# The first group of a transformer block's input projection, taken block by block of 128 channels

## The chip, the cores and the metric

The kernel runs on one core of a Trainium2 chip. The metric is the device time of one execution in microseconds. The kernel before took 1697.79 us (median of three runs, 1696.65 to 1697.9).

## The reference

One layer of an encoder block for 256 tokens of 2048 channels, in float32. Cut to what the change touches:

```python
mod = silu(c) @ w_ada + b_ada                   # 2048 -> 6 * 2048, one vector
sh1, sc1, gt1, sh2, sc2, gt2 = split(mod, 6)
h = rmsnorm(x, g_pre_mix) * (1.0 + sc1) + sh1   # 256 x 2048
proj = h @ w_in                                 # 2048 -> 10752 columns
lb = cumsum(softmax(hg_lb_logits))              # "bounds" of the forget gates
cos, sin = rotary angles of the positions       # "sines"
y = mixer(proj, lb, cos, sin)                   # gated recurrence, windowed attention, output projection
x = x + gt1 * rmsnorm(y, g_post_mix)
x = x + gt2 * rmsnorm(expert_ffn(x), g_post_ffn)  # 16 experts, each picks 32 tokens
```

## The kernel before

**Weights.** All weights come through one queue, SP's, in tiles of 128 x 2048 floats (1 MB), in the order of the list `prog` and, behind it, of the experts. `take()` (L156 to L161) issues one tile into the next free slot of a pool of 27 slots; six of these are a ring for split weights. A slot that is still read holds up the queue.

**Modulation.** `silu(c)` is spread over all partitions as a row, CR (`expand`, L293). A tile ("A", p, k) or ("B", p, k) of w_ada gives part p (0 shift, 1 scale, 2 to 5 the others) of the 128 channels of block k, by one VectorE instruction (`ada`, L398 to L401). `mod_gain` (L403) adds bias and gain.

**h.** `norm_x` (L317) squares x, scales its rows on ScalarE, turns it by 32 TensorE transposes and copies the blocks to NTl. `make_h(g)` (L411) makes h of four blocks: for each block one ScalarE instruction with scale and shift (L417), a cast to the rounded high part HH (L418), and on VectorE the low part HL, the difference (L419).

**Products.** Ten "early" chunks of 512 columns of w_in, f0 b0 f1 b1 q0 q1 hg0 hg1 v0 v1, are taken in four groups of four channel blocks each (GRP). For each chunk and group a tile ("W", ...) comes; `split` (L426 to L438) casts its two halves on ScalarE (L434) and takes the differences on VectorE (L435). `prod` (L440) issues 48 matmuls for a chunk and a group, three for each pair of block and 128 columns: high by high, high by low, low by high. The sum stands in one of two halves of PSUM (`big`, used in turn). In groups 2 to 4 ScalarE first copies the sum so far back into PSUM (L788, "reload"), and after a chunk it copies the sum out (L791, "eviction"; in group 4 L793 with a sigmoid or silu, which needs another function table). So a chunk can start only when the chunk two before has been evicted and its own sum reloaded. After the early chunks come the late chunks of w_in and the recurrence (`hgrn`), then attention, output projection, routing and the experts.

**What sets the order.** The queues of SP, and of ScalarE, VectorE and TensorE, each run their instructions in the order that a list scheduler of the framework wrote at build time; it moves instructions freely within the data dependences. `pairs` holds extra dependences that pin one instruction behind another. In the kernel before only a few are pinned: group 1's h on ScalarE, and the second square. All eight w_ada tiles of group 1 stand ahead of the first w_in tile in `prog`, then two B tiles are mixed into each group (`BE = [2, 2, 2, 10]`). Bounds and sines are computed at the very start.

Of the kernel before, what the change touches and what calls it, by code (L numbers as in the profile page):

```python
# [14 lines left out]
F32 = mybir.dt.float32  # L15
# [4 lines left out]
ALU = mybir.AluOpType  # L20
# [6 lines left out]
H = 8  # L27
NE = 16
FF = 1024
SMW = 160  # L30
# [12 lines left out]

# [81 lines left out]
def block_kernel(ctx: ExitStack, tc: tile.TileContext, x, cols, pos, ident_in, hmask, smask, w_ada, w_in, w_a, w_b, w_out, w_r, w_gu, w_dn, out):  # L125
# [35 lines left out]
        return t  # L161

    pairs = []

    def latest(engine):
        for i in reversed(nc.cur_bb.bb.instructions):
# [61 lines left out]

    NG = len(GRP)
    G0 = [sum(GRP[:g]) for g in range(NG)]  # L230
    prog = [("X",)]
    a_tiles = [("A", p, k) for k in range(KT) for p in range(2)]
    b_tiles = [("B", p, k) for p in range(2, 6) for k in range(KT)]
    prog += a_tiles[:2 * GRP[0]]
    for g in range(NG):
        todo = b_tiles[:BE[g]]
        b_tiles = b_tiles[BE[g]:]
        if g < NG - 1:
            todo = a_tiles[2 * G0[g + 1]:2 * G0[g + 1] + 2 * GRP[g + 1]] + todo
# [12 lines left out]
    def mix(items, plan):

# [26 lines left out]
    stream += [src(it) for it in prog if it[0] not in "HX"]  # L280
# [33 lines left out]
    V.tensor_tensor(sig, sig, col("c"), ALU.mult)  # L314
    CR = expand(sig, "crow")
    crow_done = latest(mybir.EngineType.Activation)
    X = [mem.get([D], F32, "x") for _ in range(NT)]  # L317
    ssq = tiny(NT)

    def norm_x():  # L320
        for tt in range(NT):
            nc.sync.dma_start(X[tt], x[tt])
        scr = mem.get([D], F32, "sq")
        for tt in range(NT):
            S.activation(scr, X[tt], AF.Square, accum_out=ssq[:, tt:tt + 1])
        pairs.append((latest(mybir.EngineType.Activation), crow_done))
        mem.put(scr)
        rs = rsqrt(ssq, NT)
        for k2 in range(8):
            if k2 % 2 == 0:  # L330
                for tt in range(NT):
                    xp = X[tt][:, 256 * k2:256 * k2 + 512]
                    S.activation(xp, xp, AF.Copy, scale=rs[:, tt:tt + 1])
            b = bank()
            for j in range(2):
                for tt in range(NT):
                    E.transpose(b[:, 256 * j + 128 * tt:256 * j + 128 * tt + 128],
                                X[tt][:, 128 * (2 * k2 + j):128 * (2 * k2 + j) + 128], ident)
            S.copy(NTl[k2 // 4][:, 2 * (k2 % 4):2 * (k2 % 4) + 2, :].rearrange("p a b -> p (a b)"), b)
        mem.put(*X)  # L340

    def load_masks():
        mtmp = mem.get([2, 128], F32, "mtmp")
# [15 lines left out]
    table()  # L359
    S.activation(le, le, AF.Exp)  # L360
    ls3 = lsum.rearrange("p (d h) -> p d h", d=2)
    V.tensor_tensor(ls3, le4[:, :, 0, :], le4[:, :, 1, :], ALU.add)
    V.reciprocal(lsum, lsum)
    V.tensor_tensor(LB, le4[:, :, 0, :], ls3, ALU.mult)
    V.tensor_scalar(OM, LB, -1.0, 1.0, ALU.mult, ALU.add)
    V.tensor_scalar(NOM, LB, 1.0, None, ALU.subtract)


    CS = cp.tile([128, 2, NT, 64], F32, name="CS")
# [1 line left out]
    def rotary():  # L371
        w = mem.get([4, 128], F32, "rot")
        ang, n_, t_ = w[:, 0, :], w[:, 1, :], w[:, 2, :]
        pf = tiny(NT)
        V.tensor_copy(pf, posi)
        for tt in range(NT):
            V.tensor_scalar(ang[:, 64 * tt:64 * tt + 64], col("inv"), pf[:, tt:tt + 1], None, ALU.mult)
        for sc in (4096.0, 1.0):
            magic = 12582912.0
            V.tensor_scalar(n_, ang, 1.0 / (2 * math.pi * sc), magic, ALU.mult, ALU.add)  # L380
            V.tensor_scalar(n_, n_, magic, None, ALU.subtract)
            for cc in (6.28125, 1.9350051879882812e-3, 3.0199159819567e-07):
# [15 lines left out]
    def ada(p, k, t):  # L398

# [11 lines left out]
    def make_h(g):  # L411
        ks = slice(G0[g], G0[g] + GRP[g])
        mod_gain(0, ks)
        mod_gain(1, ks)
        for kt in range(ks.start, ks.stop):
            n = hk(NTl, kt)
            S.activation(n, n, AF.Identity, scale=MOD[:, 1, kt:kt + 1], bias=MOD[:, 0, kt:kt + 1])  # L417
            S.copy(hk(HH, kt), n)  # L418
            V.tensor_tensor(hk(HL, kt), n, hk(HH, kt).bitcast(F32), ALU.subtract)  # L419
            if kt % 2:  # L420
                yield
        if g == NG - 1:
            mem.put(*NTl)


    def split(t):  # L426
# [430 lines left out]
    LA = LAH  # L857
    pend = []
    hs, hg_ = iter(()), 0
    for it in prog:  # L860
        if it[0] == "H":
            hs, hg_ = make_h(it[1]), it[1]
            if it[1] == 0:
                n, p = len(nc.cur_bb.bb.instructions), latest(mybir.EngineType.Activation)
                for _ in hs:
                    pass
                pairs += [(i, p) for i in nc.cur_bb.bb.instructions[n:] if i.engine == mybir.EngineType.Activation]
            continue
        if it[0] == "X":
            norm_x()  # L870
            rotary()
            continue
        t = take()
        if it[0] in "AB":
# [5 lines left out]
            if it == ("B", 4, KT - 1):  # L880
                router_consts()
        else:
            pend.append((it, split(t)))
            if it[0] == "W" and it[2] < G0[hg_]:
                next(hs, None)
            else:
                for _ in hs:
                    pass
# [398 lines left out]
```

## Time and profile before

| | |
|---|---|
| Time, median of three runs | 1697.79 us |
| Time of the profiled execution | 1695.95 us |
| Its span, first to last instruction | 1694.2 us |
| TensorE busy (matmul) | 1415.6 us, 84% |
| VectorE, ScalarE busy | 778.0 us, 554.1 us |
| DMA | 633.58 MB, mean 374 GB/s |

The span has three stretches. From 36 to about 740 us TensorE is nearly always busy with the products of the mixer; from about 750 us to the end the DMA engines are, with the experts' weights; ahead of 36 us TensorE waits for the first w_in tile. A share of busy time says little here: the change lies in the first 36 us and in the order of the ScalarE instructions up to 270 us, so single rows of the timeline are read.

### The profile page before, as it was taken

The page shows a single profiled execution, that of the slowest core. Times are in us where ns is not written, and L with a number is a line of the kernel's source. Part 1 is how long each engine was busy: PE and PEld are TensorE (multiplying, and loading weights), DVE is VectorE, ACT ScalarE, POOL GpSimd, SP SyncE. Part 2 cuts the span into 40 slices and gives each one's busy share as a digit, 9 for nine tenths or more (in the row PEclk, how much of TensorE's full clock was granted, in tenths as well). Part 3 has the DMA queues.
Part 4 walks back from the last instruction along what each step waited for, and adds up shares of the span by engine and source line. Part 5 has one row for each costly group of instructions (what it writes and reads, how often), then busy time and mean ns, then how long its engine had stood idle before and what let it go on. Part 6 is the DMA issues. An engine that isn't in the chain of part 4 may idle for free.

```text
span 1694.2 us, 22085 instructions
## 1 busy us (share of the span) xinstructions
PE 1415.6 (84%) x9162; PEld 864.6 (51%) x9162; DVE 778.0 (46%) x1070; ACT 554.1 (33%) x854; POOL 0.2 (0%) x4
## 2 busy tenths in 40 slices
PE   4999999999999999979876777776776777677776
PEld 3999997787888888853321221231222232122122
DVE  8788879989878799751111111110111111111113
ACT  6577777765675444432110100010000010001013
POOL 0000000000000000000000000000000000000000
PEclk7999999999999999998998878888987987888789
DMA  9999976665778879989999999999999999999996
GB/s 383 419 419 385 361 308 227 257 236 201 291 277 324 353 283 385 420 358 419 418 419 419 420 419 420 419 419 419 419 419 420 420 419 420 419 419 419 420 420 268
DMA packets 88372, 633.58 MB, mean 374 GB/s; under 512 B 10064, under 2 KB 10448, under 8 KB 11472
## 3 DMA queue, kind: packets, MB, share of 16 engines
q1 hardware_dynamic: 87984, 631.39, 91.8%
q8 instruction: 72, 1.18, 0.3%
q10 hardware_dynamic: 288, 0.79, 0.1%
q14 instruction: 28, 0.23, 0.0%
HBM read 630.04 MB, written 2.10 MB: 373 GB/s over the span
## 4 chain that ended last, share of the span: by engine, by line
PE 46%; DMA 46%; DVE 5%; ACT 2%; issue 1%; SPq 0%; ACTq 0%; DVEq 0%
PE PS L178 45%; DMA w<-in_w_gu_dram 33%; DMA w<-in_w_dn_dram 11%; DVE hl L435 1%; DMA w<-in_w_in_dram 1%; DMA w<-in_w_ada_dram 1%; ACT ew L1117 1%; DVE w L400 1%; DVE F L508 0%; PE PS L915 0%; PE PS L1090 0%; PE PS L686 0%; ACT ew L1087 0%; DVE T L514 0%; ACT hl L434 0%
## 5 line engine op out<-in xcount | busy, mean ns | idle before, releaser
L178 PE MATMUL PS<-w,rt 128*32 128x512 f32 x2048 | 314.4, 692 | 144.2 <-DMA w<-in_w_gu_dram 143.2
L435 DVE TENSOR_TENSOR hl<-w,hl 128x1024 fp32r<-128x1024 f32 x232 | 278.6, 1223 | 86.4 <-ACT hl L434 85.6
L178 PE MATMUL PS<-hl,hl 128*128 128x256 f32 (+1 forms) x928 | 309.3, 335 | 0.0
L434 ACT CAST hl<-w 128x1024 fp32r<-128x1024 f32 x232 | 237.7, 1049 | 151.5 <-PE PS L178 142.7
L178 PE MATMUL PS<-hl,hh 128*128 128x512 f32 x832 | 270.1, 399 | 0.7 <-ACT hl L434 0.6
L178 PEld LDWEIGHTS PS<-w,rt 128*32 128x32 f32 x2048 | 54.6, 115 | 349.0 <-DMA w<-in_w_gu_dram 283.9
L400 DVE SCALAR_TENSOR_TENSOR w<-w,crow 128x2048 f32<-128x2048 f32 x96 | 219.1, 2286 | 3.8 <-DMA w<-in_w_ada_dram 3.8
L1128 DVE TENSOR_TENSOR acc<-acc,PS 128x512 f32<-128x512 f32 x120 | 82.6, 688 | 274.2 <-PE PS L178 274.2
L178 PE MATMUL PS<-ew,rt 128*128 128x256 f32 x512 | 157.3, 434 | 60.3 <-ACT ew L1117 60.3
L178 PE MATMUL PS<-hh,hl 128*128 128x256 f32 x1024 | 186.3, 285 | 8.7 <-ACT hh L418 8.7
L178 PEld LDWEIGHTS PS<-hl,hl 128*128 128x128 f32 x928 | 177.5, 191 | 16.3 <-issue 1.0
L178 PEld LDWEIGHTS PS<-hl,hh 128*128 128x128 f32 x832 | 155.6, 188 | 33.3 <-ACT hl L434 1.0
L178 PE MATMUL PS<-w,ew 128*32 128x256 f32 x2048 | 153.2, 422 | 18.1 <-DVE ew L1096 15.4
L178 PEld LDWEIGHTS PS<-hh,hl 128*128 128x128 f32 x1024 | 161.2, 193 | 9.2 <-ACT hh L418 9.1
L178 PEld LDWEIGHTS PS<-ew,rt 128*128 128x128 f32 x512 | 94.8, 206 | 136.2 <-ACT ew L1117 121.1
L1117 ACT COPY ew<-PS 128x256 f32<-128x256 f32 x128 | 47.5, 371 | 281.4 <-PE PS L178 281.4
L1096 DVE TENSOR_TENSOR ew<-ew,PS 128x256 f32<-128x256 f32 x16 | 6.8, 422 | 230.7 <-ACT ew L1095 230.7
L178 PEld LDWEIGHTS PS<-w,ew 128*32 128x32 f32 x2048 | 57.1, 116 | 92.5 <-issue 47.4
L1087 ACT COPY ew<-PS 128x512 f32<-128x512 f32 x16 | 9.4, 585 | 226.4 <-PE PS L178 226.4
L178 PE MATMUL PS<-hl,mh 128*128 128x512 f32 x256 | 80.2, 393 | 0.0
L1051 DVE TENSOR_SCALAR rt<-ct,rt 128x128 f32<-128x128 f32 x32 | 9.6, 343 | 123.6 <-PE PS L1055 123.6
L991 DVE TENSOR_SCALAR rt<-ct,rt,small 128x32 f32<-128x32 f32 x32 | 9.4, 300 | 105.0 <-PE PS L178 104.8
(251 smaller groups left out, 1104.7 us busy)
## 6 DMA issues: line engine op xcount, KB each, us to landing
w<-in_w_gu_dram SPq DMA_DIRECT2D x256, 1024.0 KB, 19.9
w<-in_w_dn_dram SPq DMA_DIRECT2D x128, 1024.0 KB, 19.9
w<-in_w_ada_dram SPq DMA_DIRECT2D x96, 1024.0 KB, 9.0
w<-in_w_in_dram SPq DMA_DIRECT2D x84, 1024.0 KB, 7.3
w<-in_w_out_dram SPq DMA_DIRECT2D x16, 1024.0 KB, 14.6
w<-in_w_a_dram SPq DMA_DIRECT2D x8, 1024.0 KB, 7.4
w<-in_w_b_dram SPq DMA_DIRECT2D x8, 1024.0 KB, 8.2
x<-in_x_dram SPq DMA_DIRECT2D x4, 1024.0 KB, 12.4
```

Of the source, the lines that this page charges most:

```text
L178: E.matmul(o, l, r, start=start, stop=stop, skip_group_check=True, **kw)
L400: V.scalar_tensor_tensor(t, t, 1.0, CR, ALU.mult, ALU.mult, accum_out=MOD[:, p, k:k + 1])
L434: S.copy(hl[:, 0, :], w)
L435: V.tensor_tensor(hl[:, 1, :], w, hl[:, 0, :].bitcast(F32), ALU.subtract)
L991: V.tensor_scalar(oh[:, tt, :], io, pm3[:, tt, e:e + 1], r2[:, tt:tt + 1], ALU.is_equal, ALU.mult)
L1051: V.tensor_scalar(rp[:, tt], io[:, None, :].to_broadcast([128, 4, 32]), pm3[:, tt, e:e + 1], aff[:, tt, e:e + 1], ALU.is_equal, ALU.mult)
L1087: S.copy(gu, b)
L1096: V.tensor_tensor(he, sl_, b3[:, :, 64:128], ALU.mult)
L1117: S.copy(EW[:, 2, 256 * (cb % 2):256 * (cb % 2) + 256], b[:, :256])
L1128: V.tensor_tensor(acc(cb), acc(cb), p3, ALU.add)
```

## The change

The first group is written out by hand in a new function `start()`: for each block k of 128 channels the two w_ada tiles come, h of this block is made (`h_hi` on ScalarE, `h_lo` on VectorE), and the products of two chunks, f0 and b0, for this block follow (`products`), 12 matmuls per block and chunk. Their two w_in tiles stand as the third and sixth of the ten tiles; in the kernel before f0's was the ninth and b0's the eleventh. Both PSUM halves are in use for it. All instructions of `start()` on VectorE, ScalarE and TensorE are pinned in the order in which they are written. The bounds and sines move to the first chunk of group 2 ("R"), pinned behind the instructions that stand ahead there. One ScalarE table load goes at the start; `Abs` becomes a VectorE instruction. The B tiles go from 2, 2, 2, 10 to 0, 2, 2, 12 per group, and h of group 2 is made one chunk later (NH0).

```diff
-BE = [2, 2, 2, 10]
+BE = [0, 2, 2, 12]
-NH0 = 3
+NH0 = [2, 3, 3]
+    def behind(n, last):
+        for i in nc.cur_bb.bb.instructions[n:]:
+            if i.engine in last and "DMA" not in str(i.opcode):
+                pairs.append((i, last[i.engine]))
-    prog += a_tiles[:2 * GRP[0]]
+    NS = 2
+    begin = []
+    for k in range(GRP[0]):
+        begin += a_tiles[2 * k:2 * k + 2]
+        if k < NS:
+            begin.append(("W", EARLY[k], 0, GRP[0]))
...
+        names = EARLY[NS:] if g == 0 else EARLY
+        nt, ne = len(todo), len(names)
+        m = ne - 1 if g == 0 else ne
+        for i, n in enumerate(names):
             prog.append(("W", n, G0[g], GRP[g]))
+            k = min(nt, (i + 1) * nt // m) - min(nt, i * nt // m)
...
+            if g < NG - 1 and i == ne - NH0[g]:
                 prog.append(("H", g + 1))
+            if g == 1 and i == 0:
+                prog.append(("R",))
...
+    def start():
+        n0 = len(nc.cur_bb.bb.instructions)
...
+            S.copy(CR[:, 512 * c:512 * c + 512], b)
+            if c == 0:
+                S.activation(PS[:, 0:2048], X[0], AF.Square, accum_out=ssq[:, 0:1])
...
+        def h_hi(k):
+            S.activation(MOD[:, 0, k:k + 1], MOD[:, 0, k:k + 1], AF.Identity, bias=bada[:, 0, k:k + 1])
+            S.activation(MOD[:, 1, k:k + 1], MOD[:, 1, k:k + 1], AF.Identity, scale=col("gpm")[:, k:k + 1],
+                         bias=gb[:, k:k + 1])
+            n = hk(NTl, k)
+            S.activation(n, n, AF.Identity, scale=MOD[:, 1, k:k + 1], bias=MOD[:, 0, k:k + 1])
+            S.copy(hk(HH, k), n)
+        def h_lo(k):
+            V.tensor_tensor(hk(HL, k), hk(NTl, k), hk(HH, k).bitcast(F32), ALU.subtract)
+        acc = [big(), big()]
+        def products(i, k):
+            hl, _ = mod[i][k // 2]
+            j = k % 2
+            wh, wl = hl[:, 0, 512 * j:512 * j + 512], hl[:, 1, 512 * j:512 * j + 512]
+            ah, al = hk(HH, k), hk(HL, k)
+            for c in range(4):
+                o, cs = acc[i][:, 256 * c:256 * c + 256], slice(128 * c, 128 * c + 128)
+                mm(o, wh[:, cs], ah, k == 0 and c % 2 == 0, False)
+                mm(o, wl[:, cs], ah, False, False)
+                mm(o, wh[:, cs], al, False, k == 3)
...
+        one()
+        rs = rsqrt(ssq, NT, lambda: S.activation(le, le, AF.Exp))
+        scaled(0)
+        one()
+        one()
+        turn_x(0)
+        h_hi(0)
+        scaled(1)
+        turn_x(1)
+        one()
+        h_lo(0)
+        products(0, 0)
+        one()
+        one()
+        h_hi(1)
+        h_lo(1)
+        products(0, 1)
+        products(1, 0)
+        products(1, 1)
+        scaled(2)
+        turn_x(2)
+        scaled(3)
+        turn_x(3)
+        mem.put(*X)
+        one()
+        one()
+        h_hi(2)
+        one()
+        h_lo(2)
+        products(0, 2)
+        products(1, 2)
+        one()
+        h_hi(3)
+        h_lo(3)
+        products(0, 3)
+        products(1, 3)
+        new = nc.cur_bb.bb.instructions[n0:]
+        for e in (mybir.EngineType.DVE, mybir.EngineType.Activation, mybir.EngineType.PE):
+            own = [i for i in new if i.engine == e and "DMA" not in str(i.opcode)]
+            pairs.extend((i, p) for p, i in zip(own, own[1:]))
+            ends[e] = own[-1]
+        for i in range(NS):
+            S.copy(slab(EARLY[i]), acc[i])
...
+        if it[0] == "R":
+            n, last = len(nc.cur_bb.bb.instructions), {e: latest(e) for e in ends}
+            bounds()
+            next(rot)
+            behind(n, last)
             continue
```

`one()` takes the next tile: a w_ada tile for `ada`, a w_in tile for `split`. `scaled(c)` scales 512 columns of both halves of x on ScalarE, `turn_x(c)` transposes them (8 transposes on TensorE, two ScalarE copies to NTl).

The pins hold instructions of `start()` to each other, but others may come between them: on VectorE the first w_ada tile of group 2 stands ahead of the last `h_lo(3)`. The change also moves the scheduler's order further on, in three places.

The first is the turn from group 1 to group 2. On VectorE before: hl_567, hl_570 are the split of hg1, hl_628, hl_631 that of v0, the w tiles between are w_ada's, and MOD rows add bias and gain for group 2.

```order
L435 TENSOR_TENSOR hl_567<-w_565,hl_567 128x1024
L435 TENSOR_TENSOR hl_570<-w_565,hl_570 128x1024
L400 SCALAR_TENSOR_TENSOR w_623,MOD<-w_623,crow_89 128x2048
L405 TENSOR_TENSOR MOD<-MOD,ct 128x4
L407 SCALAR_TENSOR_TENSOR MOD<-MOD,ct 128x4
L435 TENSOR_TENSOR hl_628<-w_626,hl_628 128x1024
L435 TENSOR_TENSOR hl_631<-w_626,hl_631 128x1024
```

After, on VectorE: hl_620, hl_623 are the split of v0, hl_684, hl_687 that of v1.

```order
L548 TENSOR_TENSOR hl_620<-w_618,hl_620 128x1024
L548 TENSOR_TENSOR hl_623<-w_618,hl_623 128x1024
L395 SCALAR_TENSOR_TENSOR w_676,MOD<-w_676,crow_101 128x2048
L400 TENSOR_TENSOR MOD<-MOD,ct 128x4
L395 SCALAR_TENSOR_TENSOR w_679,MOD<-w_679,crow_101 128x2048
L400 TENSOR_TENSOR MOD<-MOD,ct 128x4
L402 SCALAR_TENSOR_TENSOR MOD<-MOD,ct 128x4
L548 TENSOR_TENSOR hl_684<-w_682,hl_684 128x1024
L548 TENSOR_TENSOR hl_687<-w_682,hl_687 128x1024
```

Two w_ada tiles instead of one stand ahead of the last MOD row, and this comes one chunk later, ahead of v1's split. On ScalarE before, at the same turn: Q_78 holds the sums of q0 and v0, Q_85 those of q1 and v1, F_52 those of f0 and b0; the casts are of v1 (hl_698, hl_701), f0 (hl_764, hl_767) and b0 (hl_800, hl_803), the last two for group 2.

```order
L434 CAST hl_698<-w_696 128x1024
L434 CAST hl_701<-w_696 128x1024
L791 COPY Q_78_512<-PS 128x1024
L788 COPY PS<-F_52_270 128x1024
L434 CAST hl_764<-w_762 128x1024
L434 CAST hl_767<-w_762 128x1024
L791 COPY Q_85_573<-PS 128x1024
L788 COPY PS<-F_52_270 128x1024
L434 CAST hl_800<-w_798 128x1024
L434 CAST hl_803<-w_798 128x1024
```

After, on ScalarE: Q_70 is the tile of q0 and v0, Q_77 that of q1 and v1, F_40 that of f0 and b0, hl_799 and hl_802 are b0's casts, L413 is the cast of h, L382 and L383 are the sines.

```order
L904 COPY Q_70_504<-PS 128x1024
L413 CAST hh_83<-nT_81 128x256
L382 ACT_TABLE_LOAD
L382 ACTIVATE CS<-rot_120 128x128
L383 ACTIVATE CS<-rot_120 128x128
L904 COPY Q_77_565<-PS 128x1024
L547 CAST hl_799<-w_797 128x1024
L547 CAST hl_802<-w_797 128x1024
L901 COPY PS<-F_40_350 128x1024 x2
```

The reload of f0's sum, which stood right behind v0's eviction, now stands behind v1's eviction and b0's two casts.

The second place is group 4, on ScalarE, around the eviction of q0. Before: hl_2177 and hl_2180 are the casts of q1, Q_78 is q0's sum.

```order
L793 ACTIVATE F_65_391<-PS 128x1024
L788 COPY PS<-Q_85_573 128x1024
L434 CAST hl_2177<-w_2175 128x1024
L434 CAST hl_2180<-w_2175 128x1024
L793 ACT_TABLE_LOAD
L793 ACTIVATE Q_78_512<-PS 128x1024
```

After: hl_2179 and hl_2182 are the casts of q1, Q_70 is q0's sum.

```order
L906 ACTIVATE F_57_383<-PS 128x1024
L901 COPY PS<-Q_77_565 128x1024
L906 ACT_TABLE_LOAD
L906 ACTIVATE Q_70_504<-PS 128x1024
L547 CAST hl_2179<-w_2177 128x1024
L547 CAST hl_2182<-w_2177 128x1024
```

The casts of q1 now stand behind the eviction of q0, the chunk right before it.

The third place is the end of group 4 on ScalarE. Before: Q_85 is v1's sum, hl_2486 and hl_2489 are the casts of the first late tile.

```order
L791 COPY Q_78_512<-PS 128x1024
L213 ACT_TABLE_LOAD
L504 ACTIVATE T_292_2526<-F_52_270,OM,NOM 128x256
L505 ACTIVATE F_52_270<-F_52_270,LB,OM 128x256 x4
L434 CAST hl_2486<-w_2484 128x1024
L434 CAST hl_2489<-w_2484 128x1024
L791 COPY Q_85_573<-PS 128x1024
```

After: Q_77 is v1's sum, hl_2491 and hl_2494 are the casts of the first late tile.

```order
L904 COPY Q_70_504<-PS 128x1024
L220 ACT_TABLE_LOAD
L617 ACTIVATE T_290_2531<-F_40_350,OM,NOM 128x256
L618 ACTIVATE F_40_350<-F_40_350,LB,OM 128x256 x4
L904 COPY Q_77_565<-PS 128x1024
L547 CAST hl_2491<-w_2489 128x1024
L547 CAST hl_2494<-w_2489 128x1024
```

Here too the eviction of the chunk that runs has moved ahead of the casts for the next one.

## Rows read from the trace of the kernel before

**Rows 1.** The chain that ended last, 0 to 760 us (start us, us, what).

```profile
3.53 9.12 DMA w<-in_w_ada_dram
12.72 19.87 DMA w<-in_w_in_dram
...
35.95 224.13 PE PS L178 x1704
...
267.38 11.63 PE PS L178 x50
```

**Rows 2.** A stretch of group 4: us, busy us of each engine, PEclk, DMA share, GB/s.

```profile
225.00:250.00 25.00, 25.00 (x211) 25.00 (x210) 21.05 (x21) 18.28 (x19) 0.00 (x0) 1.00 0.74 300
```

**Rows 3.** ScalarE's timeline (start us, us, ..., idle before and who ended it).

```profile
15.78 0.20 ACT L219 ACTIVATE small<-small 128x2 f32<-128x2 f32 x1
16.00 1.28 ACT L390 ACT_TABLE_LOAD   x1
...
17.52 2.54 ACT L333 ACTIVATE x<-x,small 128x512 f32<-128x512 f32 x4
19.96 1.09 ACT L339 COPY nT<-PS 128x512 f32<-128x512 f32 x2
...
34.52 1.09 ACT L417 ACTIVATE nT<-nT,MOD 128x256 f32<-128x256 f32 x2
35.51 0.69 ACT L418 CAST hh<-nT 128x256 fp32r<-128x256 f32 x2
...
49.14 1.02 ACT L791 COPY F<-PS 128x1024 f32<-128x1024 f32 x1 [2.85 <-PE PS L178]
...
77.94 1.02 ACT L791 COPY HG<-PS 128x1024 f32<-128x1024 f32 x1 [2.85 <-PE PS L178]
...
89.17 1.02 ACT L791 COPY Q<-PS 128x1024 f32<-128x1024 f32 x1 [1.99 <-PE PS L178]
90.21 1.02 ACT L788 COPY PS<-F 128x1024 f32<-128x1024 f32 x1
91.17 2.00 ACT L434 CAST hl<-w 128x1024 fp32r<-128x1024 f32 x2
94.61 1.01 ACT L791 COPY Q<-PS 128x1024 f32<-128x1024 f32 x1 [1.44 <-PE PS L178]
```

**Rows 4.** VectorE's timeline.

```profile
16.52 0.17 DVE L220 TENSOR_SCALAR small<-small 128x2 f32<-128x2 f32 x1
...
17.05 2.29 DVE L400 SCALAR_TENSOR_TENSOR w<-w,crow 128x2048 f32<-128x2048 f32 x1
...
35.98 0.75 DVE L419 TENSOR_TENSOR hl<-nT,hh 128x256 fp32r<-128x256 f32 x2
...
51.13 2.36 DVE L435 TENSOR_TENSOR hl<-w,hl 128x1024 fp32r<-128x1024 f32 x2 [1.19 <-ACT hl L434]
```

**Rows 5.** TensorE's timeline: the first transposes of x.

```profile
18.27 4.26 PE L337 MATMUL PS<-ident,x 128*128 128x128 f32 x18 [6.89 <-ACT x L333]
```

**Rows 6.** Short stretches, TensorE alone: us, busy (instructions), PEclk, DMA share, GB/s.

```profile
19.00:21.00 2.00, 2.00 (x10) 0.50 1.05 434
...
22.00:23.00 1.00, 0.53 (x3) 1.00 0.97 401
...
740.00:742.00 2.00, 2.00 (x11) 1.00 0.00 0
...
743.50:745.50 2.00, 0.00 (x0) 1.00 0.75 242
745.50:748.90 3.40, 3.17 (x14) 0.51 1.01 414
```

**Rows 7.** ScalarE around the late chunks' first cast, group 4.

```profile
265.04 1.99 ACT L434 CAST hl<-w 128x1024 fp32r<-128x1024 f32 x2
266.93 1.00 ACT L791 COPY Q<-PS 128x1024 f32<-128x1024 f32 x1
```

**Rows 8.** The page's DMA share, in tenths, in 40 equal slices of the span.

```profile
DMA  9999976665778879989999999999999999999996
```

More of the change, by code (lines that the diff above doesn't have):

```diff
@@ L29 @@
 FF = 1024
-SMW = 160
+SMW = 176
 EPS = 1e-6
@@ L278, in src @@
         return {"YA": w_a, "YB": w_b, "O": w_out}[k][it[1], it[2]]
-    stream += [src(it) for it in prog if it[0] not in "HX"]
+    stream += [src(it) for it in begin + prog if it[0] not in "HR"]
     estream = []
@@ L313, in block_kernel @@
     S.activation(sig, col("c"), AF.Sigmoid)
-    V.tensor_tensor(sig, sig, col("c"), ALU.mult)
-    CR = expand(sig, "crow")
-    crow_done = latest(mybir.EngineType.Activation)
+    table()
     X = [mem.get([D], F32, "x") for _ in range(NT)]
+    for tt in range(NT):
+        nc.sync.dma_start(X[tt], x[tt])
     ssq = tiny(NT)
[L320 to L340, printed above, removed]
     def load_masks():
@@ L423, in make_h, with one, scaled, turn_x @@
             mem.put(*NTl)
+    def start():
+        n0 = len(nc.cur_bb.bb.instructions)
+        V.tensor_tensor(sig, sig, col("c"), ALU.mult)
+        w = mem.get([4, 4, 128], F32, "diag")
+        for c in range(4):
+            V.tensor_tensor(w[:, c], ident[:, None, :].to_broadcast([128, 4, 128]),
+                            sig[:, 4 * c:4 * c + 4, None].to_broadcast([128, 4, 128]), ALU.mult)
+        for c in range(4):
+            b = bank() if c < 3 else obank
+            mm(b, ones, w[:, c].rearrange("p a b -> p (a b)"), True, True)
+            S.copy(CR[:, 512 * c:512 * c + 512], b)
+            if c == 0:
+                S.activation(PS[:, 0:2048], X[0], AF.Square, accum_out=ssq[:, 0:1])
+        mem.put(w)
+        rot = rotary()
+        next(rot)
+        S.activation(PS[:, 0:2048], X[1], AF.Square, accum_out=ssq[:, 1:2])
+        gb = tiny(4)
+        V.scalar_tensor_tensor(gb, bada[:, 1, 0:4], 1.0, col("gpm")[:, 0:4], ALU.add, ALU.mult)
+        tiles = iter(begin)
+        mod = []
+        def one():
+            it = next(tiles)
+            t = take()
+            if it[0] == "A":
+                ada(it[1], it[2], t)
+            else:
+                mod.append(split(t))
+        def scaled(c):
+            for tt in range(NT):
+                xp = X[tt][:, 512 * c:512 * c + 512]
+                S.activation(xp, xp, AF.Copy, scale=rs[:, tt:tt + 1])
+        def turn_x(c):
+            for k2 in (2 * c, 2 * c + 1):
+                b = bank()
+                for j in range(2):
+                    for tt in range(NT):
+                        E.transpose(b[:, 256 * j + 128 * tt:256 * j + 128 * tt + 128],
+                                    X[tt][:, 128 * (2 * k2 + j):128 * (2 * k2 + j) + 128], ident)
+                S.copy(NTl[k2 // 4][:, 2 * (k2 % 4):2 * (k2 % 4) + 2, :].rearrange("p a b -> p (a b)"), b)
+        def h_hi(k):
[13 more added lines that the diff above has]
+            ah, al = hk(HH, k), hk(HL, k)
+            for c in range(4):
+                o, cs = acc[i][:, 256 * c:256 * c + 256], slice(128 * c, 128 * c + 128)
+                mm(o, wh[:, cs], ah, k == 0 and c % 2 == 0, False)
+                mm(o, wl[:, cs], ah, False, False)
+                mm(o, wh[:, cs], al, False, k == 3)
+            if k % 2:
+                hring.put(hl)
+        one()
[41 more added lines that the diff above has]
+            S.copy(slab(EARLY[i]), acc[i])
+        return rot
@@ L859, in block_kernel @@
     hs, hg_ = iter(()), 0
+    rot = start()
     for it in prog:
@@ L862, in block_kernel @@
             hs, hg_ = make_h(it[1]), it[1]
[L863 to L867, printed above, removed]
-            continue
-        if it[0] == "X":
-            norm_x()
-            rotary()
+            continue
+        if it[0] == "R":
+            n, last = len(nc.cur_bb.bb.instructions), {e: latest(e) for e in ends}
+            bounds()
+            next(rot)
+            behind(n, last)
             continue
@@ L882, in block_kernel @@
         else:
+            n = len(nc.cur_bb.bb.instructions)
             pend.append((it, split(t)))
+            if it[0] == "W" and it[1:3] in ((EARLY[NS], 0), (EARLY[NS + 1], 0)):
+                behind(n, ends)
             if it[0] == "W" and it[2] < G0[hg_]:
```

29 lines of the change are left out of this document (13 added, 16 removed).

## The prediction

> **What bounds the kernel now.** I read the chain of waits first. Ahead of 36 us it hangs on two landings: the first w_ada tile lands at 12.65 us, the ninth tile, f0's, at 32.6; that is 2.49 us a tile [rows 1]. From 35.95 to 260 us it is TensorE alone. The reader is to see that there is one unbroken piece of 1704 matmuls, so that whatever makes TensorE wait inside it is paid in full, and whatever makes it start earlier is won. The stretches say the same: TensorE 25.00 of 25 us busy at the full clock, DMA at 0.74 [rows 2]. In ScalarE's timeline, evictions of chunks come 5.76 us apart ((77.94 - 49.14) / 5) and always wait for TensorE; the second chunk, b0, ends at 49.1, hg0 at 77.9, v0 at 89.1, v1 at 94.6 [rows 3]. 48 matmuls in 5.76 us are 0.12 us each.
>
> Behind the mixer the DMA engines are full to the end [rows 8], yet the delay of TensorE isn't hidden there: at 740 to 742 us they stand still, 0.00 [rows 6], since no slot is free, and start when the mixer's last work frees some. Between 270 and 740 us the DMA share is mostly below 9 tenths [rows 8], so there too the queue waits for slots and not for bandwidth. I therefore take a shift of TensorE before 270 us as a shift of the end, one for one.
>
> **The start.** Ten tiles in new order: f0 third, b0 sixth, the last w_ada tile tenth. By 2.49 us a tile f0 lands at 17.6, b0 at 25.1, the tenth at 35.1. Were landings all, f0 and b0 would end at 35.1 + 2.2 (last w_ada row on VectorE, two starts 2.2 apart [rows 4]) + 1.4 (h) + 0.4 (low part) + 2.9 (24 matmuls) = 42.0, 7.1 us earlier than 49.1. But the pinned orders form a longer chain.
> h of a block on ScalarE costs 0.2 + 0.2 + 0.55 + 0.35 = 1.3 to 1.5 us [rows 3] (the two one-column instructions aren't in the trace; between nothing and 0.3 each, 0.2 taken from the 128x2 row). ScalarE: f0's casts 17.6 to 19.6, two copies of the first transposes to 20.7, h of block 0 to 22.2, two scalings (2.54 / 4 each) to 23.5, copies of the next transposes to 26.1 (eight at 4.26 / 18 = 0.24 us [rows 5], then a copy), b0's casts to 28.1, h of block 1 to 29.6. VectorE's low part: 30.0. TensorE then has 36 products, 4.3 us at the full clock: 34.3. Only behind them, by the pins, stand the transposes of the other half of x: eight transposes and copies to 36.0, two scalings to 37.4, transposes and copies to 39.2, h of block 2 to 40.7, low part 41.1. On VectorE the eighth w_ada tile is pinned behind this (43.3), the first tile of group 2 slips in (45.6; landed at 40.1, so it doesn't wait for it), then the last low part at 46.0. 24 matmuls: 49.0. So the start wins 0.1 us: the wait for landings is replaced by a chain through all three engines. Term: 0, from -7.1 (landings alone) to +4.2 (below).
> From there on DMA keeps ahead: TensorE needs two tiles in 5.76 us, DMA brings two in 4.98.
>
> **The turn from group 1 to group 2.** In times of the kernel before, hg0 ends at 77.9. VectorE gets v0's casts at 79.9 and 80.9, ends the split at 82.2, then runs two w_ada rows (4.4) and three small ones (0.17 each): 87.1. ScalarE waits for it with h of the next group, standing ahead of v1's casts: two instructions of h (1.09), one cast (1.0), one difference (1.2, half of 2.36 [rows 4]): v1 can start at 90.4, where v0 ends at 89.1. Wait 1.35; v1 ends at 95.9. Behind that ScalarE has a cast, h, f0's casts, v0's eviction, a table load (1.28 [rows 3]) and two sines, to 97.5; v1's eviction to 98.5, b0's casts to 100.5, and only then f0's reload, to 101.5, without which f0 can't start. Before, this reload ran at 90.21 beside v1's products [rows 3]. Wait 5.65. Sum of the turn 7.0. Bounds: 0, if ScalarE were never late, to 8.0. The bounds and sines themselves save nothing at the start, where they lay in idle time, and cost here only in this queue.
>
> **Group 4.** q1's casts stand behind q0's eviction, which ends q0: eviction 1.0, cast 1.0, difference 1.2, and handing over 0.15: TensorE waits 3.35, from 0 before. At the end of group 4 the same for the first late tile: before, its casts ran at 265.04 ahead of v1's eviction at 266.93 and TensorE went on at 267.38, 0.5 after v1 [rows 1, 7]; now it waits 3.35, so 2.85 more. Bounds 0 and 3.35 for each; behind the second VectorE bounds too (its queue holds the recurrence behind the split), so it may be hidden.
> Two more B tiles in group 4 cost VectorE 2.2 us each; with one a chunk it has 1.19 us idle per chunk [rows 4], and one chunk's second tile uses this up: 0, at most 1. The queue of SP holds the same tiles; its order costs nothing while slots suffice.
>
> **The clock.** After the idle of 743.5 to 745.5 TensorE's clock was granted at 0.51 for 3.4 us [rows 6], 1.2 instead of 2.4 GHz: 1.7 lost. Three of the new waits (5.65, 3.35, 3.35) are as long; I take 1.6 each, 4.8 in all, between 0 and 7.
> The upper bound of the start rests on the same. The clock was at 0.50 during the first transposes and 1.00 from 22 us, with nothing but transposes before the rise [rows 5, 6]; so transposes and products from 23.5 to 28.4 should have raised it for the 36 products at 30.0. The Trainium skill ("TensorE: Matmul & The Clock Gate", Part 4: PE-mode transpose) says that transposes don't count as busy for the clock. This trace contradicts it. By the rule the 36 products would take 8.6 us; this is rival B.
>
> **Sum.** 0 + 7.0 + 3.35 + 2.85 + 4.8 = 18.0 us on the profiled execution's 1695.95 us (span 1694.2): 1714. That execution is 1.8 us below the median of the runs shown, 1697.79; I keep 1714, since the last wait may partly be hidden.
>
> **Rivals.**
> A, faster: the start is bound by landings alone. For it: the DMA engines are full ahead of 36 us, and all of the chain's links are short. Against it: the order of ScalarE and TensorE as written. It wins 7.1, and decides if the four later waits stay under 3.7 together, for instance if ScalarE runs ahead enough to have f0's reload done; with the group 4 waits at half a term (1.7 each without clock loss) the time is 1697.8 - 7.1 + 3.4 = 1694.1, and 1690.7 without any.
> B, the 36 products run at the lower clock: 4.3 us more at the start, and all behind it later: 1718. For it: TensorE stands idle between 28.4 and 30.0 and more than half of the time before 23.5. Against it: the rise at 22 us.
> C, the waits are there but short: the clock doesn't fall (-4.8) and the wait at the first late tile lies beside VectorE's own chain (-2.85): 1714 - 7.65 = 1706.
> D, the change does not do what it says, start and waits both stay as they were: 1697.8. For it: sum 0 of the start. Against it: f0's reload stands where it stands.
>
> **How the numbers follow.** Forecast 0.60, B 0.13, C 0.14, A 0.07, D 0.06. This kernel's runs differ by some 0.1%; no change is within 0.2%, 3.4 us. Slower holds the forecast, B and C: 0.87; D the same: 0.06; A faster: 0.07. The range from C less 3 us of the start's bounds to B plus 3 of the clock's holds about 8 in 10: 1703 to 1721.
>
> **What would show it.** The profile of the changed kernel should have: TensorE's first products near 24 to 26 us; f0's and b0's evictions near 48 and 50; idle of TensorE of 1 to 2 us ahead of v1, of 5 to 6 us ahead of group 2's f0, ended by ScalarE's copy to PSUM (L901); 3.3 us ahead of group 4's q1 and the first late tile, ended by VectorE's difference; half clock behind the longer ones; the expert stage as long as before. It would be wrong if evictions of f0 and b0 came near 42, if f0's products in group 2 followed v1's without a gap, or if the end of the mixer moved by another amount than the end of the kernel.

## The result

The changed kernel took 1709.95 us (median of four runs, 1708.79 to 1710.82), the kernel before 1697.57 beside it: 12.4 us more, ratio 1.0074 with a 95% interval of 1.0063 to 1.0086. The forecast was 1714 with a range of 1703 to 1721. Its case, four new waits of TensorE, is the one that came. By the traces its terms for these waits were 3.6 us too large, and a gain behind the mixer, 3.4 us in the run that isolates it, was not in the sum at all.

### The profile page after: what moved, and what is told of

It is laid out like the page before. It is cut to its first block, busy times and chain, and to the rows that moved or that the text cites. A ratio compares the mean times of both kernels' runs of the same rounds, so it can differ in the third digit from the quotient of the medians.

```text
span 1709.0 us, 22082 instructions
## 1 busy us (share of the span) xinstructions
PE 1417.7 (83%) x9162; PEld 863.0 (50%) x9162; DVE 777.4 (45%) x1069; ACT 556.7 (33%) x861; POOL 0.2 (0%) x4
## 4 chain that ended last, share of the span: by engine, by line
DMA 46%; PE 46%; DVE 3%; ACT 3%; issue 1%; SPq 0%; ACTq 0%; DVEq 0%
PE PS L185 44%; DMA w<-in_w_gu_dram 34%; DMA w<-in_w_dn_dram 12%; DVE hl L548 1%; DMA w<-in_w_in_dram 1%; ACT hl L547 1%; ACT ew L1231 1%; DVE w L395 0%; PE PS L1029 0%; PE PS L799 0%; DVE F L621 0%; PE PS L1204 0%; ACT nT L464 0%; ACT ew L1201 0%; PE PS L881 0%
## 5 line engine op out<-in xcount | busy, mean ns | idle before, releaser
L185 PE MATMUL PS<-w,rt 128*32 128x512 f32 x2048 | 322.2, 702 | 152.4 <-DMA w<-in_w_gu_dram 151.5
L185 PE MATMUL PS<-hh,hl 128*128 128x256 f32 x1024 | 192.4, 290 | 11.9 <-ACT PS L901 5.4
L185 PE MATMUL PS<-ew,rt 128*128 128x256 f32 x512 | 151.3, 420 | 60.4 <-ACT ew L1231 60.4
L185 PEld LDWEIGHTS PS<-hh,hl 128*128 128x128 f32 x1024 | 165.6, 198 | 13.3 <-ACT PS L901 5.8
L185 PE MATMUL PS<-w,ew 128*32 128x256 f32 x2048 | 147.8, 410 | 15.4 <-DVE ew L1210 15.4
L185 PEld LDWEIGHTS PS<-ew,rt 128*128 128x128 f32 x512 | 90.8, 197 | 132.0 <-ACT ew L1231 117.7
L1171 ACT COPY rt<-PS 128x256 f32<-128x256 f32 x16 | 6.0, 373 | 161.1 <-PE PS L1169 161.1
```

The lines of the kernel that those rows point to most:

```text
L185: E.matmul(o, l, r, start=start, stop=stop, skip_group_check=True, **kw)
L1171: S.copy(stw, b[:, :256])
```

## The profile after

The profiled execution took 1710.82 us, its span 1709.0: 14.8 more than the span before. The chain of waits of the changed kernel, 0 to 300 us (start us, us, what), against [rows 1]:

```profile
4.70 13.63 DMA w<-in_w_in_dram
...
30.00 6.25 PE PS L185 x36
...
42.32 37.08 PE PS L185 x288
...
86.19 2.22 DVE w L395 x2
...
101.44 0.92 ACT PS L901
...
102.41 144.36 PE PS L185 x1104
...
250.06 28.92 PE PS L185 x188
```

Where one piece of 1704 matmuls stood before, there are now three long ones, of 288, 1104 and 188, with gaps between them. TensorE's timeline names the gaps; the bracket at the end is its idle time before the instruction and who ended it:

```profile
102.41 0.58 PE L185 MATMUL PS<-hh,hl 128*128 128x256 f32 x1 [5.40 <-ACT PS L901]
...
248.80 0.58 PE L185 MATMUL PS<-hh,hl 128*128 128x256 f32 x1 [2.05 <-ACT hl L547]
...
281.01 0.50 PE L185 MATMUL PS<-hl,hh 128*128 128x512 f32 x1 [2.05 <-ACT hl L547]
...
282.27 0.50 PE L185 MATMUL PS<-hl,hh 128*128 128x512 f32 x1 [0.30 <-DVE hl L548]
```

These are group 2's f0, group 4's q1, and the first late tile. ScalarE's timeline around the first of them, against the rows from 89.17 on in [rows 3]:

```profile
95.53 0.99 ACT L904 COPY Q<-PS 128x1024 f32<-128x1024 f32 x1
96.43 0.40 ACT L413 CAST hh<-nT 128x256 fp32r<-128x256 f32 x1
96.85 1.28 ACT L382 ACT_TABLE_LOAD   x1
98.14 0.31 ACT L382 ACTIVATE CS<-rot 128x128 f32<-128x128 f32 x1
98.36 0.29 ACT L383 ACTIVATE CS<-rot 128x128 f32<-128x128 f32 x1
98.56 0.99 ACT L904 COPY Q<-PS 128x1024 f32<-128x1024 f32 x1
99.45 1.99 ACT L547 CAST hl<-w 128x1024 fp32r<-128x1024 f32 x2
101.34 1.96 ACT L901 COPY PS<-F 128x1024 f32<-128x1024 f32 x2
```

v1's products ended at 97.01 (102.41 less 5.40). ScalarE was busy without a pause, but with a table load, two sines, v1's eviction and b0's casts; the reload that f0 needs (L901) came last, at 101.34. Before, it ran at 90.21 beside v1's products.

The clock, in short stretches of TensorE (us, busy of PE, PEld, DVE, ACT, POOL, then the granted clock, DMA share, GB/s):

```profile
99.00:101.00 2.00, 0.00 (x0) 0.00 (x0) 1.38 (x7) 2.00 (x3) 0.00 (x0) 1.00 0.98 389
...
102.40:105.30 2.90, 2.89 (x13) 2.89 (x14) 2.90 (x4) 2.83 (x3) 0.00 (x0) 0.50 0.98 415
105.30:108.00 2.70, 2.70 (x24) 2.70 (x23) 2.70 (x3) 0.00 (x0) 0.00 (x0) 0.97 1.02 431
...
250.00:252.00 2.00, 1.96 (x10) 1.95 (x10) 2.00 (x3) 2.00 (x3) 0.00 (x0) 0.50 1.01 422
252.00:254.00 2.00, 2.00 (x18) 2.00 (x18) 2.00 (x3) 0.53 (x1) 0.00 (x0) 0.94 0.99 414
...
754.00:758.00 4.00, 4.00 (x20) 3.30 (x19) 0.00 (x0) 0.00 (x1) 0.00 (x0) 1.00 0.04 16
```

Behind each gap TensorE runs at 1.2 GHz for some 2 to 3 us, 13 matmuls in 2.9 us where 24 run in 2.7. The last row answers to 740 to 742 in [rows 6]: ahead of the mixer's end, which moved from 742.1 to 758.0, the DMA engines nearly stand still, as before.

How much each place added is read from the starts of ScalarE's 40 evictions in the two traces, whose distance is mostly 5.76 us where TensorE doesn't wait. After less before, us: group 1's hg0 +1.49 (the start), group 2's f0 +9.49 (so the turn 8.00), group 4's q0 +9.43, its q1 +13.45 (4.02), and from 300 us to the mixer's end +15.87 (so the late tile 2.4). Behind the mixer 1.1 came back.

## Experiments

All are timed beside the kernel before (1697.2 to 1697.3 in these sets). The same line has other numbers in each kernel, since edits shift them; the reload is L901 in the changed kernel and L903 to L912 in the runs. Ratios are to the kernel before; "less" is against the changed kernel where nothing else is said.

**x1_turn**, the order at the turn alone. `ready` is the reload of f0, made while v1 is taken up; the sines and v1's eviction are pinned behind it.

```diff
...
-                ps = big()
+                ps = early.pop((n, k0)) if (n, k0) in early else big()
-                if not first:
+                if not first and (n, k0) != ("f0", 4):
                     S.copy(ps, s)
+                if (n, k0) == ("v1", 0):
+                    early["f0", 4] = big()
+                    S.copy(early["f0", 4], slab("f0"))
+                    ready = latest(mybir.EngineType.Activation)
+                    pairs.extend((i, ready) for i in sines)
...
+                if (n, k0) == ("v1", 0):
+                    pairs.append((latest(mybir.EngineType.Activation), ready))
...
+            sines.extend(i for i in nc.cur_bb.bb.instructions[n:] if i.engine == mybir.EngineType.Activation)
```

> From the changed kernel, only ScalarE's order at the turn from group 1 to group 2 is pinned: f0's reload (L901) into PSUM ahead of the sines' table load and of v1's eviction. Theory S (ScalarE's order makes TensorE wait): the idle of 5.40 us ahead of group 2's f0 falls to 0.5 to 1.0, because the reload can start at about 96.9 us where v0's eviction and the last h cast are done and v1 ends at 97.0; 4.5 us less, and 6.1 if the half clock behind the idle goes too: 1704 to 1705.5. Rival V (VectorE's chain or the operands are late as well, so another wait takes its place): f0 still starts after 100.5 and the time stays above 1708.

Measured: 1702.03 us, ratio 1.0027 (1.0018 to 1.0036), 7.9 less than the changed kernel. ScalarE, and TensorE's wait ahead of f0, in its trace:

```profile
95.03 1.00 ACT L911 COPY Q<-PS 128x1024 f32<-128x1024 f32 x1
95.93 0.40 ACT L413 CAST hh<-nT 128x256 fp32r<-128x256 f32 x1
96.23 1.01 ACT L906 COPY PS<-F 128x1024 f32<-128x1024 f32 x1
97.26 1.28 ACT L382 ACT_TABLE_LOAD   x1
```

```profile
97.30 0.39 PE L185 MATMUL PS<-hh,hl 128*128 128x256 f32 x1 [0.81 <-ACT PS L906]
```

The reload stands one place ahead of the table load, and the wait is 0.81 in place of 5.40. The turn costs 2.0 in place of 8.0, the upper end of what S expected, the clock with it; by the evictions the mixer is 7.65 shorter, of which 0.5 is the start and 0.9 q1's gap, neither of which the edit touches. V is out. The time itself lies 2.0 below S's range.

**x2_g4**, the order in group 4 alone.

```diff
...
             pend.append((it, split(t)))
+            cast[it[1:3]] = latest(mybir.EngineType.Activation)
...
+                for e, c, k in (('q0', 'q1', 12), ('v1', 'akv', 0)):
+                    if last and n == e:
+                        pairs.append((latest(mybir.EngineType.Activation), cast[c, k]))
```

> From the changed kernel, only two orders in ScalarE's queue are pinned: q1's casts of group 4 ahead of q0's eviction, and the first late tile's casts ahead of v1's eviction, as the kernel before had them. Theory S: TensorE's waits of 3.26 us ahead of q1 and 3.27 ahead of the late tile go; q1 gives back 4.0 with its clock, the late tile about 1.4 to 2.5, since before it waited 1.8 there itself: 5.5 to 6.5 less, 1703.5 to 1704.5. Rival V (VectorE's split, queued behind the recurrence, is as late): the late tile gives nothing and q1 under 2, time above 1707.5.

Measured: 1702.96 us, ratio 1.0032 (1.0020 to 1.0044), 7.0 less. ScalarE at group 4's q0 and q1, first in the changed kernel, then here:

```profile
243.13 1.28 ACT L906 ACT_TABLE_LOAD   x1
246.79 1.02 ACT L906 ACTIVATE Q<-PS 128x1024 f32<-128x1024 f32 x1 [2.38 <-PE PS L185]
247.71 1.98 ACT L547 CAST hl<-w 128x1024 fp32r<-128x1024 f32 x2
```

```profile
241.17 1.99 ACT L547 CAST hl<-w 128x1024 fp32r<-128x1024 f32 x2
243.18 1.28 ACT L908 ACT_TABLE_LOAD   x1
244.92 1.02 ACT L908 ACTIVATE Q<-PS 128x1024 f32<-128x1024 f32 x1 [0.46 <-PE PS L185]
```

With the casts ahead, q1 follows q0 without a gap (evictions 5.76 apart, 9.78 in the changed kernel). The late tile keeps 0.62 + 0.47 us of waits and gives back 1.4 of its 2.4. To the other 1.0 belong two new waits in TensorE's rows, first of the kernel before, then here:

```profile
266.12 0.50 PE L178 MATMUL PS<-hl,hh 128*128 128x512 f32 x1 [0.62 <-ACT hl L434]
...
279.06 1.16 PE L178 MATMUL PS<-T,T 128*128 128x128 f32 x8
```

```profile
275.12 0.50 PE L185 MATMUL PS<-hl,hh 128*128 128x512 f32 x1 [0.47 <-DVE hl L548]
...
286.79 1.16 PE L185 MATMUL PS<-T,T 128*128 128x128 f32 x8 [1.16 <-DVE T L635]
```

TensorE now waits for VectorE, at the late tile's difference and at a tile T of the recurrence; the kernel before has neither wait. VectorE has two w_ada rows ahead of the recurrence here (267.91 and 270.12), where the kernel before has one (260.20), and in TensorE's order T stands some six matmuls earlier. Either may be the reason, the first as the price of the B tiles moved to group 4; no run undoes one of them alone. In all 5.4 is due to the pins, a little under what S expected; the time lies 0.5 below its range, V is out. This execution also started 1.9 us earlier than the one of the changed kernel, on which more below.

**x3_pins**, both edits.

> Both sets of order pins together, nothing else changed. Theory S: the gains add, 4.5 to 6.1 and 5.5 to 6.5, so 1697.5 to 1700, with what is left over the kernel before being the start (1.5 us) and the wait ahead of v1 (1.2). Rival G (a gain at the turn is given back later, because group 2 to 4 then wait for loads or slots): evictions of group 3 are no earlier than in the kernel with the second set alone, and the sum falls short by 3 us or more.

Measured: 1696.05 us, ratio 0.9993 (0.9985 to 1.0002). The gains 7.9 and 7.0 add to 14.9, and 13.9 came; evictions of group 3 and 4 stay as far ahead as at the turn. G is out. By the evictions the two pieces of order in ScalarE's queue account for 11.4 of the 14.4 us of waits (turn 6.0, q1 4.0, late tile 1.4); the mixer is still 3.8 us longer than in the kernel before. That the time came out no longer than that kernel's, and 1.5 below S's range, was the first sign of a gain elsewhere.

**x4_noR** undoes the move of bounds and sines.

```diff
-            bounds()
-            next(rot)
-            behind(n, last)
...
         for i in range(NS):
             S.copy(slab(EARLY[i]), acc[i])
+        bounds()
+        next(rot)
```

> Undoes one part: the bounds and the sines stand in the start's stretch again, as before; all else as in the changed kernel. Theory S: the table load and two sines (1.28 + 0.3 + 0.3 us) no longer stand ahead of v1's eviction, the reload of f0 follows that eviction directly with no casts between, so f0 starts about 97.0 + 2.1 + ... near 99.2 instead of 102.4: 2.5 to 4 us less, 1706 to 1707.5; the start stays at +1.5. Rival B (the sines moved away had freed the start): f0's and b0's first evictions come 1 us or more later than 49.2 and 51.0 and the time is 1710 or above.

Measured: 1704.15 us, ratio 1.0039 (1.0026 to 1.0052), 5.8 less. ScalarE here:

```profile
96.53 1.01 ACT L906 COPY Q<-PS 128x1024 f32<-128x1024 f32 x1 [0.20 <-PE PS L185]
97.44 1.97 ACT L903 COPY PS<-F 128x1024 f32<-128x1024 f32 x2
```

f0 starts at 98.52, behind a wait of 2.02, and the turn costs 4.7 in place of 8.0: as theory S has it, 3.3 less. Group 4 keeps its 4.1. b0's eviction comes at 50.54, so B is out. The mixer is 3.5 shorter; the median says 5.8, 1.9 below S's range. The rest I can't account for: the five runs scatter from 1702.38 to 1706.2, the profiled one being the slowest, and the stage behind the mixer was 1.1 shorter than in the changed kernel's trace.

**x5_pins_h**, h of group 2 behind v1's casts as well.

```diff
+            if kt == G0[1]:
+                last = latest(mybir.EngineType.Activation)
             S.activation(n, n, AF.Identity, scale=MOD[:, 1, kt:kt + 1], bias=MOD[:, 0, kt:kt + 1])
+            if g == 1:
+                pairs.append((latest(mybir.EngineType.Activation), last))
```

> Both sets of order pins, and one more: ScalarE's four h instructions of group 2 (L412) stand behind v1's casts instead of two of them ahead. What is left at the turn in the kernel with both sets of pins is 2.0 us: 1.2 of TensorE's wait ahead of v1, since those h instructions wait for two w_ada rows on VectorE until 88.05 and v1's casts stand behind them, and 0.8 ahead of f0. Theory S (ScalarE's order): the 1.2 goes and the 0.8 shrinks or stays, so 1.2 to 2 less than the 1696.05 of that kernel: 1694 to 1695. Rival V (VectorE's chain is the bound at the turn: it ends the two w_ada rows at 87.85 and splits v1 only then, and h comes later for f0): the wait moves from v1 to f0, nothing gained, 1695.5 to 1697.

Measured: 1695.16 us, ratio 0.9989 (0.9980 to 0.9998). ScalarE at the turn:

```profile
85.05 2.00 ACT L551 CAST hl<-w 128x1024 fp32r<-128x1024 f32 x2
87.77 1.09 ACT L414 ACTIVATE nT<-nT,MOD 128x256 f32<-128x256 f32 x2 [0.73 <-DVE MOD L402]
...
92.87 1.00 ACT L917 COPY Q<-PS 128x1024 f32<-128x1024 f32 x1
93.91 1.02 ACT L912 COPY PS<-F 128x1024 f32<-128x1024 f32 x1
```

v1's casts run at 85.05, ahead of the h that waits for VectorE until 87.77, and the turn costs 0.2 in place of 2.0: S, not V. The mixer is 2.1 shorter than with x3's pins. By medians the gain is 0.9, smaller than the scatter of either kernel's runs; so the trace decides this one, not the time.

**x6_start**: x5, and the start's orders. v0's eviction is pinned behind v1's casts as well, so that the earlier start doesn't turn these round again.

```diff
-        products(0, 1)
-        products(1, 0)
-        products(1, 1)
         scaled(2)
+        products(0, 1)
         turn_x(2)
         scaled(3)
+        products(1, 0)
         turn_x(3)
+        products(1, 1)
         mem.put(*X)
         one()
         one()
         h_hi(2)
         one()
+        one()
         h_lo(2)
         products(0, 2)
         products(1, 2)
-        one()
         h_hi(3)
...
             ada(it[1], it[2], t)
+            if it == ("A", 0, 4):
+                behind(n, ends)
```

> The kernel with all these pins, and the start's orders changed: the transposes of the second half of x and their scalings stand between the first products instead of behind all of them, the last w_ada tile's row is issued ahead of the last two low parts, and the first w_ada row of group 2 stands behind the start. Theory S: the start hangs on its pinned chain through ScalarE, TensorE and VectorE and not on landings (tenth tile at 35.1, row to 37.4, h 39.0, low part 39.8, 24 products): f0 and b0 end near 43.5 to 45 instead of 50.3, 5 to 6.5 less than the kernel with the pins alone: 1688 to 1690. Rival L (the start is bound by landings or by VectorE's rows): f0 and b0 end within 1 us of 50.3, time within 1.5 of the kernel with the pins. Rival V (VectorE, with less time for group 1's eight splits and eight rows, makes the turn wait instead): f0 and b0 end early, but the turn gives back 3 us or more, 1692 to 1694.

Measured: 1689.83 us, ratio 0.9961 (0.9947 to 0.9975): 7.5 less than the kernel before and 5.3 less than x5. b0's eviction, first in the changed kernel, then here:

```profile
51.05 1.01 ACT L535 COPY F<-PS 128x1024 f32<-128x1024 f32 x1
```

```profile
44.84 1.02 ACT L539 COPY F<-PS 128x1024 f32<-128x1024 f32 x1 [0.42 <-PE PS L185]
```

In x5 it came at 50.05, but there and in the changed kernel it stands behind a cast of ScalarE and not behind TensorE. hg0's eviction is the better measure: 78.38 in x5, 73.64 here, so the start won 4.7 us, and the turn still costs 0.2. L and V are out: the start hung on its pinned chain. Which of the changed orders gave how much wasn't tested one by one. This is the best kernel of the study.

**x7, x8, x9, x10**: the gain behind the mixer. In the kernel before, the stage from the mixer's end to the end of the span lasted 952.1 us, in the changed kernel 951.0, in x1, x2 and x3 948.5 to 948.9, with the same bytes.

> The kernel before once more, for one question: in the traces taken so far the stage behind the mixer, where the DMA engines are full, lasted 952 us in the kernel before (419 to 420 GB/s) and 948.5 to 951 in the changed kernel and the ones with pins (421 GB/s). Theory K (something in the changed kernel makes that stage shorter): this run shows 419 to 420 GB/s and 951.5 to 952.5 again. Theory R (it differs from run to run): 421 GB/s and 948.5 to 950.5 can occur here too.

> The kernel before with one number changed: SMW (line 30), the width of a small constant tile, 176 in place of 160, as the changed kernel has it. No instruction is added or moved; every tile behind that one in SBUF, the slots of the weight tiles among them, lies 64 bytes further in each partition (byte 288 of every 512 becomes 352). Theory A (the place of the slots sets the rate of the full DMA engines): the stage behind the mixer runs at 421 GB/s in place of 419 and lasts 949 instead of 952.4 us, the mixer stays, the time falls by 3 us to about 1694.2. Theory O (something in the order of the changed kernel's work shortens that stage): 419 GB/s and 1697.3 as before.

> The changed kernel with SMW 192 in place of 176, nothing else: the slots lie at byte 416 of every 512, which is 32 past a multiple of 128, as the kernel before's 288 is; 352 is 96 past one. Theory A, in the form that the place within 128 bytes counts: 419 GB/s and a stage behind the mixer of about 952 us, 3 more than with 176. In the form that any other place than 288 is as good, or by theory O: 421 GB/s and 949 to 951.

> The kernel with the pins and the new start, SMW 184: the slots lie at byte 384 of every 512, a multiple of 128. Theory A: if 96 past a multiple of 128 runs better than 32 past one, a multiple itself could run better still or the same: 421 GB/s or more, 1687 to 1690.5. Theory O: no difference from the 1689.83 of the same kernel with 176.

x8 is this, in the kernel before, and x9 and x10 the like with 192 and 184 in place of the changed kernel's 176:

```diff
-SMW = 160
+SMW = 176
```

Measured: x7 1696.6 us (one run); x8 1693.89, ratio 0.9979 (0.9970 to 0.9988), 3.4 less than the kernel before; x9 1708.67 (one run); x10 1691.11, ratio 0.9962 (0.9949 to 0.9974), as x6 within their intervals and 0.6 above the range expected. The stretch of 800 to 1600 us, where the DMA engines are full (the columns of the short stretches above), in the kernel before, in x7, in x8 and in the changed kernel:

```profile
800.00:1600.00 800.00, 587.20 (x4324) 203.01 (x4320) 113.41 (x199) 70.05 (x169) 0.00 (x0) 0.87 1.01 419
```

```profile
800.00:1600.00 800.00, 590.72 (x4300) 198.65 (x4298) 113.26 (x199) 68.94 (x167) 0.00 (x0) 0.86 1.01 419
```

```profile
800.00:1600.00 800.00, 590.93 (x4342) 204.17 (x4340) 113.67 (x200) 71.70 (x172) 0.00 (x0) 0.87 1.01 421
```

```profile
800.00:1600.00 800.00, 583.74 (x4394) 199.57 (x4387) 113.50 (x200) 74.69 (x177) 0.00 (x0) 0.89 1.01 421
```

x8 has the order of the kernel before and the rate of the changed one, so K is right and O is out: the place of the tiles, 64 bytes further, decides. Each of x8's 11 runs is faster than each of the 15 of the kernel before beside it. x9 and x10 show 421 as well: of the four widths tried (160, 176, 184 and 192, which put the slots at byte 288, 352, 384 and 416 of every 512 by the count in the expectations) only the kernel before's is slower, and 384, a multiple of 128, is no better than the others. The stage lasted 952.5 us in x7 and 948.9 in x8 (span less the mixer's end, 1692.7 - 743.8), 3.2 less than before. By the rates, rounded as they are, 2 in 420 of 950 us would be 4.5. In x9 it lasted 951.5 and in x10 950.5 in spite of the 421: 421 alone doesn't make the stage as short as in x8, on which more below. No run has the changed kernel's order with the old width, so what the 64 bytes are worth there isn't measured.

## Why the prediction was right, and where it was not

**The turn.** Predicted 7.0 and a clock loss of 1.6; measured 8.0 with the clock. The wait ahead of f0 was 5.40 (predicted 5.65), and that ahead of v1 0.9 (1.35): v1's products ended at 97.01, where hg1's eviction at 85.19 and two chunks of 5.44 give 96.07. The chain was as written out, reload last. x1 shows the cause, x5 the smaller half.

**Group 4's q1.** Predicted 3.35 and 1.6; measured 4.02. The mechanism is shown by x2. What was too large is the clock, and x1 tells the two apart: it has the same order here, but its clock stayed at 1.00. Its rows:

```profile
242.36 0.38 PE L185 MATMUL PS<-hh,hl 128*128 128x256 f32 x1 [2.05 <-ACT hl L547]
243.62 0.50 PE L185 MATMUL PS<-hh,hl 128*128 128x256 f32 x2 [0.52 <-DVE hl L548]
```

With these two waits q1 cost 3.09 (evictions 8.85 apart), near the 3.35. So the half clock, at 0.50 to 252 us in the changed kernel, added 0.9 and not 1.6: the first four matmuls, which need only the cast, took 1.22 us there (248.80 to 250.02), and the second wait was gone.

**The late tile.** Predicted 2.85 more and 1.6 of clock; measured 2.4, of which x2 shows only 1.4 to be the casts' order. This is the step that failed most. I counted eviction, cast and difference, 3.35 us, and took 0.5 for the wait of the kernel before, from the eviction at 266.93; but that eviction stands behind the casts, and TensorE had gone on at 266.12 after 0.62. TensorE needs only the cast to go on: its wait was 2.05 + 0.30. For chunks of this kind the low part comes later in the product, and the difference lies beside the first three matmuls. The clock was at 0.50 here too, from 284 to 286 us; but part of all this delay cost nothing, since x2, without it, waits 0.47 and 1.16 for VectorE. So rival C's condition, that the wait lies beside VectorE's own chain, was met in part. The 1.0 that x2 doesn't give back may be the price of the B tiles of group 4, for which I took 0, at most 1; that isn't shown.

**The start.** Predicted 0; +1.49 in this execution. The traces show no effect of the change on it beyond their spread: hg0's eviction came at 77.94, 78.23 and 79.69 us in the three traces with the old start, 78.6 in the mean, and at 79.43, 78.94, 77.57, 78.65, 78.93, 78.38 and 77.09 in the seven with the new one (x1 to x5 and x9 with the changed kernel; x4's has the bounds and sines in it), 78.4. The chain ran as written out up to the 36 products, which began at 30.00 as forecast. The spread of 2 us in the new start has two sources: when f0's tile lands (17.42 to 18.33 us in the seven), and the clock at the 36 products. The first rows, from the idle ahead of the products on, are of the changed kernel, the last is of x2:

```profile
28.00:29.90 1.90, 0.00 (x0) 0.00 (x0) 1.85 (x2) 1.83 (x6) 0.00 (x0) 1.00 0.99 414
30.00:31.50 1.50, 1.50 (x7) 1.34 (x8) 1.50 (x2) 1.19 (x2) 0.00 (x0) 0.62 1.01 421
31.50:33.00 1.50, 1.50 (x9) 1.50 (x9) 1.50 (x3) 0.00 (x0) 0.00 (x0) 0.50 1.02 426
```

```profile
31.10:32.60 1.50, 1.50 (x15) 1.50 (x14) 1.50 (x3) 0.00 (x0) 0.00 (x0) 1.00 1.00 415
```

The 36 products took 6.25 us there and 4.81 here; 6.14 to 6.29 in x1, x3, x4 and x5, and 4.80 in x9. So rival B was nearly half right in five of the seven traces, 1.9 of its 4.3 us: the clock had risen for the products, as forecast, but fell again within them. The Trainium skill's rule on PE-mode transposes ("TensorE: Matmul & The Clock Gate", Part 4), as the prediction reads it, would have had all 36 at 1.2 GHz, 8.6 us by the prediction's estimate; no run shows that, but 12 products stand between the transposes and these, so it is no clean test of the rule. Rival A is refuted as stated: of the landings only f0's, the third tile's, at 18.33 us bounds the start, and the rest is the pinned chain. Yet x6 shows that 4.7 of its 7.1 us were there to be had by another order.

**Where the sum came together.** In the profiled executions 18.0 was predicted for 14.8 measured: the turn 0.6 less, q1 0.9, the late tile 2.1, the start 1.5 more, and 1.1 back behind the mixer. "A shift of the end, one for one" held up to the mixer's end: from 320 to 560 us the shift stands at 15.8 to 15.9. Then the mixer's end moved by 15.9 and the kernel's by 14.8, which the prediction names as a sign of being wrong: it held the stage behind the mixer for unchanged, and the change's SMW, 160 to 176, shortens it, by 3.4 us in x8. The changed kernel's trace shows less of it (951.0 in place of 948.8). Part of that lies right behind its mixer, from 772 to 830 us, where the DMA engines ran at 412 GB/s; x4, x9 and x10 have the same stretch (408 to 411), x1, x2, x3 and x6 don't (421), x5 and x8 lie between (416, 419). At 421 that stretch would be 1.2 us shorter. Why is open. By medians: 8.0 + 4.0 + 2.4 - 3.4 = 11.0, of 12.4 measured with an interval of 10.7 to 14.6.

So the mechanism was right and the sum too large: waits 3.6 us too large and a gain of 3.4 us unseen both push it up, and 18.0 is 5.6 above the median's 12.4. That 1714 is only 4.0 above 1709.95 is in part luck, since the 18.0 were added to an execution 1.6 us faster than the median of the kernel before. The best kernel's 7.5 us are nearly half the unseen gain, and for the rest the start's order. x8 against x5 (1693.89 and 1695.16) suggests that the change as made, its three orders mended, gains nothing but the 64 bytes.

## What to carry over

When a change adds work to an engine that isn't the bottleneck, list what stands in its queue ahead of each instruction that the bottleneck waits for: here a table load and an eviction, each a place too early, cost some 11 us, and a few pinned orders gave them back. Size a wait by what the next instruction on the bottleneck needs, and ask what it would wait for next if that came earlier (here the late tile's cast, then VectorE). And look for constants in the diff that move memory: a width raised by 16 floats was worth nearly a third of that.

## What was unexpected of the hardware

- With the same instructions in the same order, tiles that lie 64 bytes further in each partition were filled at 421 GB/s in place of 419 by full DMA engines. 419 was seen in both traces of the kernel before, 421 with each of the three other widths. That another tile than the slots makes the difference isn't excluded, since all tiles behind that one move.
- TensorE's clock fell while it stood idle or a little later, not at the wait's beginning: in the 5.40 us gap it was granted at 1.00 from 99 to 101 us and at 0.50 from 102.4 on, when the work came back; ahead of the 36 products it was 1.00 in the idle stretch and fell to 0.50 within them. Behind the same gap of 2.05 us ahead of group 4's q1 it was granted at 0.50 in the changed kernel, x4 and x9, and stayed at 1.00 in x1.
- The new start, up to hg0's eviction, differs by 2.3 us between seven executions of kernels that share it (77.09 to 79.43), as much as some of the terms argued about here.
